# Moving the operands of a down-projection by 32 bytes in the on-chip memory

## The chip, the cores and the metric

The kernel runs on one core of a Trainium2 chip. The metric is the device time of one execution in microseconds (us); the time before is the median of three runs. Beside the runs there is one profiled execution, whose trace gives every duration used below. PE is the matrix engine (TensorE), PEld its weight loads, DVE the vector engine, ACT the scalar engine, POOL the GpSimd engine, SP the engine that issues most DMAs.

## The reference

One inference step of one trunk layer, for a prompt of 2048 tokens and a sample of 64 tokens (2112 in all), model width 1024. What matters here is the second half of the layer, a gated feed-forward block with a short causal convolution and a down-projection from 2816 to 1024 columns:

```python
h2 = rmsnorm(x, g2) * (1 + sc2) + sh2
up = h2 @ w_up                                   # 1024 -> 2 * 2816
conv = b_conv + sum(w_conv[j] * upp[:, j:j + T] for j in range(3))
a, g = jnp.split(conv, 2, -1)
x = x + gt2 * ((jax.nn.silu(g) * a) @ w_down)    # 2816 -> 1024
y = rmsnorm(x, g_final)
```

The first half (pooling mixer, matrix memory, output projection) takes roughly the first 790 us of the span and does not touch the tiles of this change.

## The kernel before, in words

Numbers are float32. Every large product is made from three passes over a number split in a high and a low part (weight high by operand high, weight high by operand low, weight low by operand high; `PASSES` in the code). So an operand tile holds two planes, `[P, 2, width]`, plane 0 the high part and plane 1 the low part.

The tokens are worked through in three groups of 704 (`FT`), each as two halves of 352 (`FH`). For each group the 22 blocks of 128 hidden columns are made one after the other by `Pair.products` (seven products of 352 columns each, line L1594, from the operand tiles `hx`), then convolved and gated on DVE, ACT and POOL, and split by ACT and DVE into an operand tile `av` of the down-projection. The down-projection has two forms:

- `down` (L2160): a row block of the output over the columns 0 to 448 and 448 to 704 of the group (`ENDS`), that is, matmuls of 448 and of 256 columns; 816 of each. It is used for all parts of the first group and for the last part of the two other groups.
- `quad_down` (L2037): four hidden blocks at a time by a seven-product scheme, in matmuls of 352 columns; 1344 of them, in the second and third groups.

`down_end` and `rows_add` (L2009) add the products from PSUM to the residual rows `x0` to `x7`. At the very end `final_end` (L1920), called once for the columns before 448 and once for those behind, forms the final norm: column sums on PE (L1935), the reciprocal root in the small tile `rs` (L1891, L1893), its spreading (L1951) and the last products with the rows.

The order of the instructions on PE, ACT, DVE and POOL is written out by hand in this half of the kernel (`tc.manual_schedule`); DMAs are issued by SP.

Where the tiles lie: the pool `f2` is filled from the upper end of the on-chip memory downwards. It holds, in this order of address, `OC`, `x0` to `x3`, seven `av` tiles of 5632 bytes (22 times 256), `x4` to `x7`, and on top the buffers of `rs`, of which each takes 32 bytes. So the size of the `rs` buffers sets where all that lies below them begins. In the built program before, each `av` tile begins 160 bytes past a multiple of 256. Its two planes are 2816 bytes apart (11 times 256), and the second part of 256 columns of `down` begins 1792 bytes in (7 times 256), so all operands of L2160 begin at 160 as well. In the tiles of `quad_down` two operands of 352 columns (1408 bytes, five and a half times 256) stand behind each other in a plane: the lower begins at 160, the upper at 32 past a multiple of 256; 672 matmuls read the one kind, 672 the other.

For comparison, the other operands: a row of `hx` is padded so that its 352 columns begin 128 bytes past a multiple of 256 (`HX, HO = 2 * 384, 32`); the operands `hl` and `mx` of the first half begin on multiples of 256, and so do all the split weights `wt`.

Of the kernel before, what the change touches and what calls it, by code (L numbers as in the profile page):

```python
# [9 lines left out]
F32 = mybir.dt.float32  # L10
# [6 lines left out]
P = 128  # L17
# [47 lines left out]
def tile_layer(ctx: ExitStack, tc: tile.TileContext, xT, vecs, cst, rst, w_mod, w_ada, w_qkou, w_v, w_pool,  # L65
# [21 lines left out]
    def m2_ps():  # L87
        return bank("m2")
# [580 lines left out]
    def fscr(dt=F32):  # L669
        if dt in ("rb", "ssum"):  # L670
            return spare[0].tile([P, FT], F32, tag=dt, name=dt)
        return spare[0].tile([P, FT], dt, tag="fscr", name="fscr", bufs=4)
# [855 lines left out]
    f2 = fctx.enter_context(tc.tile_pool(name="f2", bufs=1, side="right"))  # L1528
# [357 lines left out]
    def stat_cols(ps, out, tiles):  # L1886

        nf = sum(1 for t in tiles if t == P)
        for (a, b, n) in ((0, nf, P), (nf, len(tiles), tiles[-1])):
            if a < b:  # L1890
                dve.tensor_scalar(out=out[:n, a:b], in0=ps[:n, a:b], scalar1=1.0 / D, scalar2=EPS,  # L1891
                                  op0=ALU.mult, op1=ALU.add)
                pool.tensor_tensor(out=out[:n, a:b], in0=out[:n, a:b], in1=half[:n, :b - a], op=ALU.pow)  # L1893
# [26 lines left out]
    def final_end(o, x3, sums, lo, hi):  # L1920

        w = hi - lo
        tiles = [(t, min(P, hi - t)) for t in range(lo, hi, P)]
        for _ in range(4 if lo == 0 else 0):
            yield
        ps = m2_ps()
        rs = f2.tile([P, 5], F32, tag="rs", name="rs", bufs=2)
        order = [(ti, i) for ti in range(len(tiles)) for i in range(len(sums))]
        if lo > 0:
            order.sort(key=lambda c: c[1])  # L1930
        if lo > 0:
            dve.memset(ps[:, :len(tiles)], 0.0)
        for ti, i in order:
            (t, n), (sq, base) = tiles[ti], sums[i]
            pe.matmul(ps[:n, ti:ti + 1], sq[:, t - base:t - base + n], ones[:, 0:1], start=(i == 0 and lo == 0), stop=(i == len(sums) - 1),  # L1935
                      skip_group_check=lo > 0)

        if lo > 0:
            late[0](YLATE)
        stat_cols(ps, rs, [n for (t, n) in tiles])  # L1940
        if lo > 0:
            late[0](KD)
        else:
            for _ in range(4):
                yield

        def spread():

            pb = m2_ps()
            for ti, (t, n) in enumerate(tiles):  # L1950
                pe.matmul(pb[:, t - lo:t - lo + n], rs[:n, ti:ti + 1].broadcast_to([n, P]), ident[:n, :n], start=True, stop=True)  # L1951
            return pb
        pb = spread()

        if lo > 0:
            pc, rb = spread(), fscr()
            act.activation(rb[:, :w], pc[:, :w], AF.Copy)
        YG = ((0, 1), (1, 3), (3, 5), (5, 6), (6, 8))
        y = {}
        for (a, b) in YG:  # L1960
            if a % 2 == 0 or b - a == 2:
                t = f1.tile([P, 2, HX], F32R, tag="hx", name="y", bufs=2 * len(BN)).bitcast(F32).rearrange(
                    "p a t -> p (a t)")[:, :3 * w].rearrange("p (k t) -> p k t", t=w)
                j = 0
            for k in range(a, b):
                y[k] = (t, j)
                j += 1

        def store(a, b):
            (nc.sync if a < 5 else nc.scalar).dma_start(  # L1970
                out=yT[a:b, :, o.t0 + lo:o.t0 + hi].rearrange("k p t -> p k t"), in_=y[a][0][:, y[a][1]:y[a][1] + b - a, :w])

        def rows(upto):
            while due and due[0] < upto:
                k = due.pop(0)
                dve.tensor_tensor(out=y[k][0][:, y[k][1], :w], in0=x3[k][:, lo:hi], in1=pb[:, :w], op=ALU.mult)
                for (a, b) in YG:
                    if b == k + 1:
                        store(a, b)
        due = list(range(KD))  # L1980
        if lo == 0:
            late.append(rows)
            for k in range(KD - 4):
                rows(k + 1)
                yield
                yield
            return
        for k in (6, 7):
            pool.tensor_tensor(out=y[k][0][:, y[k][1], :w], in0=x3[k][:, lo:hi], in1=rb[:, :w], op=ALU.mult)
        due[6:] = []  # L1990
        rows(KD)
        store(6, 8)
        yield
# [117 lines left out]
    for o in fgroups:  # L2111
        Bo = B[o.g]
        held = None
        for pi, part in enumerate(PARTS[o.g]):
# [99 lines left out]
            for secs in [(c,) for c in ENDS] if ends else (ENDS,):  # L2214
                sums = [(ssum, 0)]
                for n in range(NE, KD):
                    ps = [take() for _ in secs]
                    down(ps, rows[n], range(nf), secs, ends)
                    down_end(n, ps, secs)
                if ends:  # L2220
                    bg[0].append(final_end(o, x3, sums, *secs[0]))
# [92 lines left out]
```

## Time and profile before

| | us |
|---|---|
| median of 3 runs | 2173.73 |
| the runs | 2172.52 to 2175.91 |
| the profiled execution's own time | 2174.68 |
| its span, first to last instruction | 2172.9 |
| PE busy | 2151.4 (99%) |
| granted TensorE clock, mean | 0.998 |

In a group's row the figures are: times it occurs, busy time of the group (overlapping instructions counted once), mean length of one instruction, and idle time of the engine just before. Matmuls are pipelined: one of 352 columns is some 320 ns long in the trace while the next starts about 160 ns after it. What a stream of matmuls costs is the distance from one start to the next, called its pace here. It can be read from a row of the timeline, which gives the first start, the stretch to the last end, and the count: (stretch less the length of the last one) by (count less one).

### The profile page before, as it was taken

To read this page: it belongs to the slowest core of one execution; us is meant where nothing else is said; L and a number is where in the kernel's file an instruction comes from. 1 tells how busy PE (TensorE), PEld (TensorE's weight loads), DVE (VectorE), ACT (ScalarE), POOL (GpSimd) and SP (SyncE) were. 2 spreads that over 40 slices of the span, in tenths; PEclk is the share of its full clock that TensorE was granted. 3 is DMA by queue.
4 is the path that set the end of the run, shared out by engine and by line. 5 is a ranking of instruction groups with operands and counts; after the bars stand their busy time and mean duration, and the time that the engine had idled before them with its cause. 6 is when DMAs were issued, how large, how long until landed. Compare 5 with 4: busy or idle time off the path is not lost.

```text
span 2172.9 us, 38060 instructions
## 1 busy us (share of the span) xinstructions
PE 2151.4 (99%) x13553; PEld 2044.4 (94%) x13553; DVE 1634.9 (75%) x3040; ACT 1096.1 (50%) x2181; POOL 258.4 (12%) x475
## 2 busy tenths in 40 slices
PE   8999999999999999999999999999999999999998
PEld 7888888888899999999999999999999999999998
DVE  5878668667955778797967668888886597887874
ACT  4554335334333446464736445655655365565554
POOL 0010000001000201010101220100101321111112
PEclk9999999999999999999999999999999999999999
DMA  8987997987888477888967976666668675555542
GB/s 319 328 305 233 323 321 246 309 302 244 301 283 288 169 260 239 282 292 300 350 214 255 321 245 222 234 208 209 228 222 274 223 255 186 170 177 190 171 160 77
DMA packets 297351, 539.51 MB, mean 248 GB/s; under 512 B 25760, under 2 KB 114336, under 8 KB 297160
## 3 DMA queue, kind: packets, MB, share of 16 engines
q1 hardware_dynamic: 286568, 511.87, 69.6%
q10 hardware_dynamic: 10592, 25.20, 3.0%
q8 instruction: 107, 1.75, 0.3%
q14 instruction: 84, 0.69, 0.1%
HBM read 410.98 MB, written 125.98 MB: 247 GB/s over the span
## 4 chain that ended last, share of the span: by engine, by line
PE 85%; DMA 5%; DVE 5%; issue 2%; ACT 2%; SPq 0%; POOL 0%; DVEq 0%; ACTq 0%; POOLq 0%
PE mm L1594 34%; PE mm L478 22%; PE mm L2160 12%; PE mm L2037 8%; PE mm L1133 3%; DVE wt L414 1%; DMA wt<-wsum 1%; PE m L1323 1%; DMA hl_kept<-wt 1%; PE m L1308 1%; PE m L1343 1%; PE m L1345 1%; DVE tg L1572 1%; DMA raw<-w_qkou 0%; ACT wt L411 0%
## 5 line engine op out<-in xcount | busy, mean ns | idle before, releaser
L1594 PE MATMUL mm<-hx,wt 128*128 128x352 f32 x5544 | 885.9, 321 | 0.7 <-DVE wt L414 0.5
L1594 PEld LDWEIGHTS mm<-hx,wt 128*128 128x128 f32 x5544 | 878.7, 188 | 2.6 <-DVE wt L414 2.0
L478 PE MATMUL mm<-hl,wt 128*128 128x512 f32 (+2 forms) x1920 | 387.4, 357 | 0.0
L411 ACT ACTIVATE wt<-raw 128x512 fp32r<-128x512 f32 (+3 forms) x470 | 276.6, 597 | 177.6 <-PE mm L478 52.8
L478 PEld LDWEIGHTS mm<-hl,wt 128*128 128x128 f32 x1920 | 316.4, 189 | 47.7 <-issue 4.4
L414 DVE TENSOR_TENSOR wt<-raw,wt 128x512 fp32r<-128x512 f32 (+3 forms) x470 | 312.8, 672 | 61.9 <-ACT wt L411 61.7
L2160 PE MATMUL mm<-av,wt 128*128 128x448 f32 (+1 forms) x1632 | 262.7, 322 | 0.0
L2160 PEld LDWEIGHTS mm<-av,wt 128*128 128x128 f32 x1632 | 250.4, 188 | 11.1
L2009 DVE SCALAR_TENSOR_TENSOR x<-mm,MOD,x 128x352 f32<-128x352 f32 (+3 forms) x360 | 167.5, 505 | 77.7 <-PE mm L2160 64.3
L2037 PE MATMUL mm<-av,wt 128*128 128x352 f32 x1344 | 220.7, 323 | 1.9 <-DVE x L2009 0.7
L2037 PEld LDWEIGHTS mm<-av,wt 128*128 128x128 f32 x1344 | 215.4, 188 | 5.0 <-DVE ea L1603 3.0
L1641 ACT ACTIVATE mm<-mm 128x352 f32<-128x352 f32 x196 | 87.8, 448 | 233.7 <-PE mm L1594 177.1
L478 PE MATMUL mm<-mx,wt 128*128 128x512 f32 (+1 forms) x960 | 182.9, 352 | 0.3 <-DVE scr L250 0.3
L478 PEld LDWEIGHTS mm<-mx,wt 128*128 128x128 f32 x960 | 159.4, 188 | 23.0 <-PE mm L478 0.5
L1572 DVE SCALAR_TENSOR_TENSOR ta<-ea,V,ta 128x704 f32<-128x704 f32 (+1 forms) x132 | 125.7, 953 | 58.4 <-ACT ta L1567 54.4
L1572 DVE SCALAR_TENSOR_TENSOR tg<-eg,V,tg 128x704 f32<-128x704 f32 (+1 forms) x132 | 125.7, 952 | 56.8 <-ACT tg L1567 54.3
L414 DVE TENSOR_TENSOR wt<-wt 128x512 fp32r<-128x512 f32 x196 | 133.0, 685 | 12.8 <-ACT wt L411 12.7
L411 ACT ACTIVATE wt<-wt 128x512 fp32r<-128x512 f32 x196 | 119.2, 622 | 36.6 <-DMA wt<-wsum 35.7
L1550 POOL COPY ea<-UC 128x2 f32<-128x2 f32 x66 | 33.1, 501 | 506.2 <-DVE ta L1572 407.3
L1781 ACT ACTIVATE tg<-tg 128x704 f32<-128x704 f32 (+1 forms) x66 | 52.5, 795 | 71.8 <-DVE tg L1572 71.8
L1133 PE MATMUL mm<-wt,hl 128*128 128x256 f32 (+1 forms) x576 | 71.4, 284 | 0.0
L1133 PEld LDWEIGHTS mm<-wt,hl 128*128 128x128 f32 x576 | 70.4, 190 | 0.8 <-issue 0.6
(305 smaller groups left out, 2207.0 us busy)
## 6 DMA issues: line engine op xcount, KB each, us to landing
wt<-wsplit SPq DMA_DIRECT2D x132, 512.0 KB, 4.3
raw<-w_up SPq DMA_DIRECT2D x198, 256.0 KB, 3.8
wt<-hl_kept SPq DMA_DIRECT2D x96, 512.0 KB, 6.3
wt<-wsum SPq DMA_DIRECT2D x132, 256.0 KB, 5.0
wsplit<-wt SPq DMA_DIRECT2D x66, 512.0 KB, 5.1
w<-w_up SPq DMA_DIRECT2D x88, 256.0 KB, 4.4
wsum<-w SPq DMA_DIRECT2D x44, 512.0 KB, 5.9
Bd<-fscr ACTq DMA_DIRECT2D x56, 352.0 KB, 4.3
```

What stands on the lines that cost most here:

```text
L411: act.activation(u.w[:, 0, :u.n], u.raw[:, :u.n], AF.Copy)
L414: dve.tensor_tensor(out=u.w[:, 1, :u.n], in0=u.raw[:, :u.n], in1=u.w[:, 0, :u.n].bitcast(F32), op=ALU.subtract)
L478: pe.matmul(ps[bi][:, :hi - lo], U[:, a, k % 4 * P:(k % 4 + 1) * P], mv[k][:, b, lo:hi], start=(at == 0 and pi == 0), stop=(k == order[-1] ...
L1133: pe.matmul(ps[ti][:n, :cols], h[4 * kh + k4][:, b, lo:lo + n], U[:, a, k4 % 2 * cols:(k4 % 2 + 1) * cols], start=(kh == 0 and k4 == 0 and ...
L1550: pool.tensor_copy(ext[:, 0:2], UC[:, f, :])
L1572: dve.scalar_tensor_tensor(out=t[:, :E], in0=ext[:, j:j + E], scalar=wc(j, f), in1=t[:, :E], op0=ALU.mult, op1=ALU.add)
L1594: pe.matmul(bk.t[:, :FH], U[:, a, kc * P:(kc + 1) * P], Bo.at(nm, kc, b), start=(first and kc == 0 and pi == 0), stop=(kc == 3 and pi == 2 ...
L1641: act.activation(to.t[:, :FH], bk.t[:, :FH], AF.Copy)
L1781: act.activation(self.tg[:, :E], self.tg[:, :E], AF.Silu)
L2009: dve.scalar_tensor_tensor(out=x3[n][:, a:b], in0=bk.t[:, a - lo:b - lo], scalar=gt2(n, s), in1=x3[n][:, a:b], op0=ALU.mult, op1=ALU.add)
L2037: pe.matmul(bk.t[:, :FH], U[:, a, c:c + P], quad.put(op, m, b), start=(first and m == 0 and pi == 0), stop=(m == 1 and pi == 2), skip_grou ...
L2160: pe.matmul(bks[i].t[:, :hi - lo], U[:, a, k % 4 * P:(k % 4 + 1) * P], av[k][:, b, lo:hi], start=(k == 0 and (a, b) == PASSES[0]), stop=(k ...
```

## The change

The tile `rs` gets three buffers in place of two. It is allocated twice, so the third buffer is never used; it only takes 32 bytes at the top of the pool.

```diff
@@ -1924,7 +1924,7 @@ def final_end(o, x3, sums, lo, hi)
         for _ in range(4 if lo == 0 else 0):
             yield
         ps = m2_ps()
-        rs = f2.tile([P, 5], F32, tag="rs", name="rs", bufs=2)
+        rs = f2.tile([P, 5], F32, tag="rs", name="rs", bufs=3)
         order = [(ti, i) for ti in range(len(tiles)) for i in range(len(sums))]
```

In the built program `OC`, `x0` to `x7`, the `av` tiles (which also hold the raw quarter weights `qs` in the first group) and one of the two `rs` buffers begin 32 bytes lower; every other tile stays where it was. The operands of L2160 and the lower ones of L2037 now begin 128 past a multiple of 256, the upper ones of L2037 on a multiple of 256. No instruction, wait or DMA is added, removed or moved on any engine.

## The prediction

> **What bounds the kernel now.** The page comes first: its line of busy times says which engine fills the span.
>
> ```profile
> span 2172.9 us, 38060 instructions
> PE 2151.4 (99%) x13553; PEld 2044.4 (94%) x13553; DVE 1634.9 (75%) x3040; ACT 1096.1 (50%) x2181; POOL 258.4 (12%) x475
> ```
>
> PE is busy 99% of the span and no other computing engine above 75%. The change touches no instruction, only where some operands begin, so the question is which instructions read or write the shifted tiles and how long PE waits around them. The groups by line and form, and the list of what PE waited for between 858 and 2153 us (the stretch in which the shifted tiles are read by matmuls), give that:
>
> ```profile
> L2160 PE MATMUL mm<-av,wt 128*128 128x448 f32 x816 | 178.8, 363 | 0.0
> L2160 PE MATMUL mm<-av,wt 128*128 128x256 f32 x816 | 111.0, 280 | 0.0
> L2037 PE MATMUL mm<-av,wt 128*128 128x352 f32 x1344 | 220.7, 323 | 1.9 <-DVE x L2009 0.7 <-DVE wt L414 0.4 <-DVE ea L1603 0.3
> L1594 PE MATMUL mm<-hx,wt 128*128 128x352 f32 x5544 | 885.9, 321 | 0.7 <-DVE wt L414 0.5
> ...
> PE mm L2037 <- DVE x L2009: 0.7, 1, 0.7
> PE mm L1594 <- DVE wt L414: 0.5, 2, 0.3
> PE mm L2037 <- DVE wt L414: 0.4, 1, 0.4
> PE mm L2037 <- DVE ea L1603: 0.3, 1, 0.3
> ```
>
> The reader sees 2976 matmuls (816 + 816 + 1344) that read `av`, and PE idle for 0.0, 0.0 and 1.9 us before them: the stream is bound by its own pace, not by a supplier. The last part of the chain of waits agrees:
>
> ```profile
> 2111.97 3.87 PE mm L2160 x24
> 2115.84 1.90 PE mm L1594 x12
> 2117.74 34.92 PE mm L2160 x204
> ```
>
> So a nanosecond more or less per matmul of `av` goes to the end of the kernel nearly whole: 1 ns on all of them is 3.0 us. The measure of what counts: 0.2% of this kernel, 4.35 us, is about what a measurement of it can tell from no change.
>
> **The paces.** Rows of the timeline in stretches with one kind of matmul (start, stretch to the last end, form, count):
>
> ```profile
> 2130.96 17.97 PE L2160 MATMUL mm<-av,wt 128*128 128x448 f32 x89
> 2148.97 3.45 PE L2160 MATMUL mm<-av,wt 128*128 128x256 f32 x28
> 1331.03 14.25 PE L2037 MATMUL mm<-av,wt 128*128 128x352 f32 x88
> 1199.76 6.50 PE L1594 MATMUL mm<-hx,wt 128*128 128x352 f32 x40
> 174.94 25.32 PE L478 MATMUL mm<-mx,wt 128*128 128x512 f32 x111
> 588.00 5.68 PE L1133 MATMUL mm<-wt,hl 128*128 128x256 f32 x46
> 867.91 2.64 PE L2160 MATMUL mm<-av,wt 128*128 128x448 f32 x12
> 870.51 1.36 PE L2160 MATMUL mm<-av,wt 128*128 128x256 f32 x10
> ...
> L478 PE MATMUL mm<-mx,wt 128*128 128x512 f32 x576 | 131.3, 389 | 0.0
> ```
>
> Taking off the length of the last one (363, 280, 323, 321 and 389 ns by form; for L1133 I use 280 too) and dividing by the count less one:
>
> - 448 columns from 160 past a multiple of 256: (17.97 - 0.363) / 88 = 200.1 ns
> - 352 columns from 160 or 32: (14.25 - 0.323) / 87 = 160.1 ns
> - 512 columns from a multiple: (25.32 - 0.389) / 110 = 226.6 ns
> - 352 columns from 128 (`hx`): (6.50 - 0.321) / 39 = 158.4 ns
> - 256 columns from 160: (3.45 - 0.280) / 27 = 117.4 ns
> - 256 columns from a multiple (L1133): (5.68 - 0.280) / 45 = 120.0 ns
>
> The first three lie on one line. From 352 to 448 columns the pace grows by 40.0 ns, from 448 to 512 by 26.5 ns, both 0.415 ns a column, and what is left over at no columns is about 13.4 ns (160.1 - 352 x 0.4167). I call this the fixed part. For `hx`, with the same 352 columns but a start at 128, it is 11.7 ns, for the 256 columns from 160 it is 10.7 ns, for those from a multiple 13.3 ns. The last two rows of the fence are a stretch in which the same L2160 ran slower: (2.64 - 0.363) / 11 = 207.0 ns for 448 columns, fixed part 20.3 ns, and (1.36 - 0.280) / 9 = 120.0 ns for 256. So the fixed part is not a constant: rows of this trace show 10.7 to 20.3 ns, and the same start address (160) appears with 10.7, 13.4 and 20.3.
>
> **The change part by part.**
>
> *The third buffer.* It costs no instruction, and no wait goes: `rs` is allocated twice and had two buffers. Price 0.
>
> *The lower operands of L2037, 160 to 128: 672 matmuls.* The nearest row is exact: `hx` has 352 columns from 128 and the same kind of weights, and paces 158.4 ns. 672 x (158.4 - 160.1) = -1.1 us. Bounds: 0 if the pace of `hx` comes from something other than its start, -1.8 us if the fixed part falls to the 10.7 ns of the 256-column row.
>
> *The upper operands of L2037, 32 to 0: 672 matmuls.* No row has 352 columns from a multiple of 256. The 512-column row from a multiple has the fixed part that these matmuls already have. I take 0; bounds -1.8 us and, by the slow stretch, 672 x 6.9 = +4.6 us.
>
> *The 448-column matmuls of L2160, 160 to 128: 816.* No row has them at 128. The nearest by start is `hx`, whose fixed part is 1.7 ns below the line: 816 x -1.7 = -1.4 us. Bounds: -2.2 us (fixed part 10.7), +5.6 us (all at the 207.0 ns of the slow stretch).
>
> *The 256-column matmuls of L2160, 160 to 128: 816.* They are already below the line. With the start of `hx` they may stay (0) or go to the 120.0 ns of the row from a multiple, +2.1 us; the fixed part of `hx` would be 118.4, +0.8 us. I take 0, since nothing in the trace shows 256 columns from 128.
>
> *What else touches the shifted tiles.* ACT and DVE write `av`, DVE and POOL read and write `x`. Rows of the same size on shifted and unshifted tiles:
>
> ```profile
> L1813 DVE TENSOR_TENSOR av<-tg,av 128x704 fp32r<-128x704 f32 x32 | 28.3, 885 | 0.1
> L1786 DVE TENSOR_TENSOR tg<-ta,tg 128x704 f32<-128x704 f32 x28 | 24.8, 884 | 3.3 <-ACT tg L1781 3.3
> L1910 DVE SCALAR_TENSOR_TENSOR x<-x,V,rb 128x704 f32<-128x704 f32 x16 | 15.1, 946 | 0.0
> L737 DVE SCALAR_TENSOR_TENSOR fscr<-fscr,G,rb 128x704 f32<-128x704 f32 x8 | 7.6, 946 | 0.0
> ```
>
> 885 against 884 and 946 against 946 ns, although `fscr` begins on a multiple of 256 and `tg` at three other offsets: the start does not move these engines, and a nanosecond there would lie beside PE anyway. The DMAs into `x` and `qs` land long before use (no wait of PE above names them). Price 0; were a row operation of DVE slower, PE waits of the 0.7 us kind (L2037 on L2009) would grow first.
>
> *Sum.* -1.1 + 0 - 1.4 + 0 = -2.5 us against the profiled execution's own 2174.68 us, giving 2172.2. That execution lies 1.0 us above the median of the runs, so the median would be 2173.73 - 2.5 = 2171.2 us. What is late next if PE is this much faster: DVE's weight splits (the 0.5 and 0.4 us on L414 above); spread over 1300 us, 2.5 us does not reach them.
>
> The Trainium skill has a rule that speaks against any effect: "TensorE: Matmul & The Clock Gate", section "Back-to-back issue gap", gives the distance of two warm matmuls as columns divided by 2.4 plus 2.5 ns, with no term for where an operand begins. By it 352 columns would pace 149.2 ns and the change would be worth 0. The trace's column cost agrees with it (0.415 ns), its fixed part of 10.7 to 20.3 ns does not.
>
> **The rivals.**
>
> *No effect.* The fixed part has nothing to do with the start, and `hx` is faster for another reason (other tiles, other order of planes). For it: the start 160 stands beside three different fixed parts, and the starts 160 and 32 pace alike in L2037. Against it: the one stream that begins at 128 is the one 352-column stream below the line, with 5544 matmuls in it. Time: 2173.7. In the Trainium skill, "SBUF — State Buffer", section "Door 1: The DMA port swizzle", tells of lines of 16 bytes, within which accesses run at full rate; 160, 128, 32 and 0 are all multiples of 16, so this rule too makes no difference between them. No row here can show it.
>
> *Faster by more.* Once the start is on a multiple of 128, the streams on the line drop to the lowest fixed part that the trace shows, 10.7 ns: 1344 x -2.7 = -3.6 us in L2037 and 816 x -2.7 = -2.2 us for 448 columns, together -5.8 us: 2167.9. For it: `hx` at 128 has gone more than half of that way. Against it: the 512 columns from a multiple are on the line.
>
> *Slower.* The slow stretch shows that the stream of L2160 can run in a longer pace with nothing else changed. If the new starts put it there for good, 448 columns cost 816 x 6.9 = +5.6 us and 256 columns 816 x 2.6 = +2.1 us, less the 1.1 us of L2037: +6.6 us, 2180.3. It passes 0.2% once some seven tenths of the L2160 matmuls run so ((4.35 + 1.1) / 7.7). For it: the two paces, 200.1 and 207.0, exist side by side at the same start. Against it: the slow stretch is short and falls back on its own, and `hx` at 128 keeps its short pace in the row above.
>
> **How the numbers follow.** Forecast (-2.5 us, within 0.2%): 0.33. No effect (within 0.2%): 0.12. Faster by more: 0.31. Slower: 0.24. This gives faster 0.31, same 0.45, slower 0.24. The forecast's own range, from the bounds of its terms without the slow stretch, is -5.8 to +2.1 us; the range must take in the faster rival (2167.9, so 2167.0) and most of the slower one. Stopping at 2179.0 leaves out its far end, about 1 in 10, and below 2167 about as much. The likeliest case alone would be 2167.9 to 2175.8.
>
> **What would show it right or wrong.** In the profile after, the timeline rows of the same stretches: L2037 should show a mix of 158.4 and 160.1 ns (mean 159.3), L2160 some 198.4 ns for 448 columns and 117.4 for 256, `hx` unchanged at 158.4 and the 512 columns at 226.6. The busy time of the L2037 group should fall from 220.7 by about 1 us, that of L2160 (178.8 and 111.0 by form) by about 1.4 together. The forecast is wrong if the 448 columns pace 207 (slower), if all are near 197 and 157 (faster by more), if nothing moves (no effect), or if the time moves while these paces stand still, which would put the cause in a transfer or a row operation that I priced at 0.

## The result, and the profile after

The changed kernel takes 2181.19 us at the median of 7 runs (2176.14 to 2182.84), the kernel before 2173.35 us (2170.73 to 2175.91): a ratio of 1.0033, 95% interval 1.0024 to 1.0043. It is slower by some 7 to 8 us, where the prediction had -2.5 us. Two executions in the batches below, one of the kernel before (2345.53 us) and one with only L2160 moved to 128 (5509.18 us), took far longer than all others and are left out of every median and ratio.

The profiled execution after has a span of 2181.1 us, 8.2 us more than before. The groups by line and form, with busy time of the group behind the bar, then the mean length of one:

```profile
span 2181.1 us, 38060 instructions
L1594 PE MATMUL mm<-hx,wt 128*128 128x352 f32 x5544 | 892.5, 322 | 0.0
L2037 PE MATMUL mm<-av,wt 128*128 128x352 f32 x1344 | 220.0, 323 | 1.5 <-DVE x L2009 0.4 <-DVE wt L414 0.4
L2160 PE MATMUL mm<-av,wt 128*128 128x448 f32 x816 | 180.8, 366 | 0.0
L2160 PE MATMUL mm<-av,wt 128*128 128x256 f32 x816 | 112.1, 282 | 0.0
```

Against the rows of before: L2037 went down by 0.7 us, the 448 columns up by 2.0, the 256 columns up by 1.1. But the largest step is in L1594, +6.6 us, and L1594 reads `hx`, which the change does not move. PE still waits for nothing there. Adding up the distances from each matmul's start to the next gives the same account: L1594 +6.0 us, 448 columns +2.0, 256 columns +0.8, L2037 -1.1, all other matmuls +0.1 on balance, together 7.8 of the 8.2 us.

The paces, as in the prediction, from timeline rows after (start, stretch, form of the first, count):

```profile
2139.16 17.91 PE L2160 MATMUL mm<-av,wt 128*128 128x448 f32 x87
2157.63 3.00 PE L2160 MATMUL mm<-av,wt 128*128 128x256 f32 x24
1339.18 14.01 PE L2037 MATMUL mm<-av,wt 128*128 128x352 f32 x87
901.75 18.49 PE L1594 MATMUL mm<-hx,wt 128*128 128x352 f32 x110
1011.74 18.49 PE L1594 MATMUL mm<-hx,wt 128*128 128x352 f32 x110
1141.72 18.53 PE L1594 MATMUL mm<-hx,wt 128*128 128x352 f32 x116
1368.75 18.53 PE L1594 MATMUL mm<-hx,wt 128*128 128x352 f32 x116
```

Stretch less the last length, by the count less one: 204.0 ns for 448 columns (before 200.1), 118.3 for 256 (117.4), 159.2 for L2037 (160.1). The last four rows are the finding: the same L1594 paces (18.49 - 0.322) / 109 = 166.7 ns in the second and third long stretch of the first group and (18.53 - 0.322) / 115 = 158.3 ns from the fourth on. Before, the second and third ran at 158.3 too:

```profile
900.76 18.53 PE L1594 MATMUL mm<-hx,wt 128*128 128x352 f32 x116
1007.73 18.53 PE L1594 MATMUL mm<-hx,wt 128*128 128x352 f32 x116
```

So a stream of `hx` has two paces, a short one of 158.3 ns and a long one of 166.7. The two long stretches hold 408 and 492 matmuls; 900 x 8.3 ns = 7.5 us. Some 2 us of that were won back, since short breaks that stood in these stretches before are gone in the slower stream. The granted TensorE clock from 800 to 1250 us, where both stretches lie, is 1.00 in both traces, so a lower clock is not the reason.

Both paces were already there before the change; near the beginning of the first group 64 matmuls of `hx` ran in the long one:

```profile
793.85 10.82 PE L1594 MATMUL mm<-hx,wt 128*128 128x352 f32 x64
```

(10.82 - 0.321) / 63 = 166.7 ns. The prediction did not use this row.

### The profile page after: what moved, and what is told of

It is laid out like the page before. It is cut to its first block, busy times and chain, and to the rows that moved or that the text cites. A ratio compares the mean times of both kernels' runs of the same rounds, so it can differ in the third digit from the quotient of the medians.

```text
span 2181.1 us, 38060 instructions
## 1 busy us (share of the span) xinstructions
PE 2160.3 (99%) x13553; PEld 2053.1 (94%) x13553; DVE 1634.9 (75%) x3040; ACT 1096.4 (50%) x2181; POOL 259.6 (12%) x475
## 4 chain that ended last, share of the span: by engine, by line
PE 90%; DVE 4%; DMA 3%; issue 1%; ACT 1%; SPq 0%; POOL 0%; DVEq 0%; POOLq 0%; ACTq 0%
PE mm L1594 37%; PE mm L478 23%; PE mm L2160 12%; PE mm L2037 8%; PE mm L1133 3%; DVE wt L414 1%; PE m L1323 1%; PE m L1343 1%; PE m L1345 1%; DMA hl_kept<-wt 1%; PE m L1308 1%; DMA raw<-w_ada 1%; DVE tg L1572 0%; ACT tg L1567 0%; PE mm L1069 0%
## 5 line engine op out<-in xcount | busy, mean ns | idle before, releaser
L1594 PE MATMUL mm<-hx,wt 128*128 128x352 f32 x5544 | 892.5, 322 | 0.0
L1594 PEld LDWEIGHTS mm<-hx,wt 128*128 128x128 f32 x5544 | 886.5, 188 | 0.5 <-DVE wt L414 0.5
L2160 PE MATMUL mm<-av,wt 128*128 128x448 f32 (+1 forms) x1632 | 265.8, 324 | 0.0
L2160 PEld LDWEIGHTS mm<-av,wt 128*128 128x128 f32 x1632 | 251.7, 188 | 12.9
L2037 PE MATMUL mm<-av,wt 128*128 128x352 f32 x1344 | 220.0, 323 | 1.5 <-DVE x L2009 0.4
L2037 PEld LDWEIGHTS mm<-av,wt 128*128 128x128 f32 x1344 | 214.8, 188 | 4.6 <-DVE ea L1603 2.8
L478 PEld LDWEIGHTS mm<-mx,wt 128*128 128x128 f32 x960 | 159.3, 188 | 22.7 <-PE mm L478 0.2
```

What stands on the lines that cost most here:

```text
L478: pe.matmul(ps[bi][:, :hi - lo], U[:, a, k % 4 * P:(k % 4 + 1) * P], mv[k][:, b, lo:hi], start=(at == 0 and pi == 0), stop=(k == order[-1] ...
L1594: pe.matmul(bk.t[:, :FH], U[:, a, kc * P:(kc + 1) * P], Bo.at(nm, kc, b), start=(first and kc == 0 and pi == 0), stop=(kc == 3 and pi == 2 ...
L2037: pe.matmul(bk.t[:, :FH], U[:, a, c:c + P], quad.put(op, m, b), start=(first and m == 0 and pi == 0), stop=(m == 1 and pi == 2), skip_grou ...
L2160: pe.matmul(bks[i].t[:, :hi - lo], U[:, a, k % 4 * P:(k % 4 + 1) * P], av[k][:, b, lo:hi], start=(k == 0 and (a, b) == PASSES[0]), stop=(k ...
```

## The experiments

One theory, A, stood against three rivals at first. A: the start of an operand within 256 bytes sets the pace of its own stream, and a stream of `hx` goes on in the phase in which the stream before it left PE. Rivals: the place of the tiles in the memory as such (B), the operands of L2037 or the rows `x` (C), or work that runs beside the `hx` stream and is slowed by the new places (called A2 below).

The experiments ran in three batches on different chips, each with the kernel before beside it; ratios are against the kernel before of the same batch, whose median was 2174.35, 2175.90 and 2174.53 us. Paces come from one profiled execution of each kernel, times from 4 to 11 executions.

In the experiments on one kind of operand, each `av` tile is 256 bytes longer, so that its start can be chosen by use, while all other tiles move by multiples of 256 bytes only:

```diff
+    def av_tile(name, off):
+        t = f2.tile([P, 2 * FT + 64], F32R, tag="av", name=name, bufs=AVB)
+        return t[:, off:off + 2 * FT].rearrange("p (a t) -> p a t", a=2)
```

`split_hi` (operands of L2160) and `Quad.put` (of L2037) take their own `off`, in steps of 8 numbers (32 bytes) from a base at 160; `x0` to `x7` stay at 160.

**All tiles 256 bytes lower.**

```diff
-        rs = f2.tile([P, 5], F32, tag="rs", name="rs", bufs=2)
+        rs = f2.tile([P, 5], F32, tag="rs", name="rs", bufs=10)
```

> Ten rs buffers in place of two: all shifted tiles lie 256 bytes lower than before, with the same starts past a multiple of 256 (160 and 32). Theory A (the pace of the matmul streams is set by the start of the operand within 256 bytes, and by the pace in which a stream is entered): all paces as before, the hx stretches of the first group at 158.3 ns, about 2173.4 us. Rival B (the place of the tiles in the memory as such, or the number of buffers, matters): slower than before as the change is, 2181 us.

Measured: 2175.46 us, ratio 1.0002 (0.9993 to 1.0012). The mean distance of starts, breaks left out, was 201.2 ns for 448 columns and 117.5 for 256, and the three `hx` stretches were entered at 158.3 (the first of them took up 166.7 for its last hundred matmuls, behind one distance of 197 ns, without a change in what it reads). The place as such and the number of buffers do nothing; rival B falls.

**Only the operands of L2160 at 128, and only those of L2037 at 128 and 0.**

```diff
-            self.d = f2.tile([P, 2, FT], F32R, tag="av", name="av", bufs=AVB)
+            self.d = av_tile("av", 56)        # only L2160; Quad.put has 0
...
-                self.tiles[key] = f2.tile([P, 2, FT], F32R, tag="av", name="av", bufs=AVB)
+                self.tiles[key] = av_tile("av", 56)     # only L2037; split_hi has 0
```

> Only the operands of L2160 begin at 128 past a multiple of 256; those of L2037 stay at 160 and 32, and x0 to x7 at 160. Theory A (L2160 at 128 paces worse itself, and leaves PE in the long pace when the hx stretch behind it begins): nearly the whole loss, hx at 166.7 ns in the two long stretches of the first group, 448 columns at 203.7 ns on the mean, 2179 to 2182 us. Rival C (the loss comes from the operands of L2037 or from the shifted rows x): 2172 to 2175 us.

> Only the operands of L2037 begin at 128 and 0 past a multiple of 256; those of L2160 stay at 160, and x0 to x7 at 160. Theory A: hx as before at 158.3 ns, L2160 as before at 201.2 ns for 448 columns, L2037 at 160 ns (half at 159), about 2172 to 2174 us. Rival C (the loss comes from the operands of L2037): 2179 to 2182 us.

Measured: only L2160, 2180.72 us, ratio 1.0030 (1.0017 to 1.0044), which is the whole loss with L2037 and `x` unmoved; only L2037, 2174.45 us, ratio 1.0001 (0.9992 to 1.0010). Rival C falls. In the trace of the first, L1594 took 4.9 us more than before, the 448 columns 2.0 and the 256 columns 0.9. In the second run L2037 went from 160.2 to 159.7 ns on the mean, breaks left out, and the `hx` stretches were entered in the short pace, though two of them took up the long one later.

The trace of the first of the two shows more than was asked. Its second long stretch, with idle time and its releaser in brackets:

```profile
897.60 4.16 PE L1594 MATMUL mm<-hx,wt 128*128 128x352 f32 x24
902.00 44.29 PE L1594 MATMUL mm<-hx,wt 128*128 128x352 f32 x278 [0.25 <-ACT mm L1641]
946.51 16.78 PE L1594 MATMUL mm<-hx,wt 128*128 128x352 f32 x100 [0.22 <-DVE wt L414]
946.78 3.80 PE L1594 MATMUL mm<-hx,wt 128*128 128x352 f32 x23
950.80 12.49 PE L1594 MATMUL mm<-hx,wt 128*128 128x352 f32 x74
```

24 matmuls pace (4.16 - 0.322) / 23 = 166.9 ns; then PE waits 0.25 us, and the next 278 pace (44.29 - 0.322) / 277 = 158.7. Here the pace changed across a break. Then PE waits 0.22 us, but that break does not bring the long pace back. The last two rows are narrower windows of the third: behind the break 23 matmuls still pace (3.80 - 0.322) / 22 = 158.1, then one distance between starts is 207 ns, with no idle time on record, and from there the pace is (12.49 - 0.322) / 73 = 166.7. The operands' places are the same throughout this stretch. The pace of `hx` is a state of the stream and not a property of its operands alone.

What switches it is not settled. In the thirteen traces with `hx` at 128, 67 places inside `hx` stretches have a distance of more than 190 ns between two starts, with at least eight matmuls on either side (places closer than ten matmuls counted as one). Behind 56 of them the short pace goes on. The longest wait among these, in the run with only the operands of L2037 moved, is ahead of this row:

```profile
1066.29 15.96 PE L1594 MATMUL mm<-hx,wt 128*128 128x352 f32 x99 [0.80 <-DVE wt L414]
```

Its mean distance is (15.96 - 0.322) / 98 = 159.6 ns, with one of 265 right behind the wait. Behind ten of the 67 places the long pace follows the short one: seven have distances of 194 to 265 ns and no idle time on record, three have 0.18 to 0.57 us of it. Behind one, the wait of 0.25 us above, the short pace follows the long. With only L2160 at 128 the long pace also begins at 1477 us with no distance over 170 ns near it.

**The changed kernel with a break ahead of the stretch.**

```diff
             b1 = self.b1 = take()
+            if o.g == 0 and f > 0 and self.i == 0:
+                for _ in range(4):
+                    pe.matmul(b1.t[:, 0:1], ones, ones[:, 0:1], start=True, stop=True)
```

> The changed kernel with four one-column products on PE, of a tile of ones into the bank about to be overwritten, ahead of the first product of each of the three hx stretches of the first group that follow a down-projection; some 0.4 us each. Theory A1 (the pace is a state that a stream inherits from what ran before it, and a break in the stream ends it): the two long hx stretches run at 158.3 ns in place of 166.7, that is 900 matmuls by 8.3 ns, -7.5 us, less 1.3 us for the products and some 2 us of waits that come back: 2176 to 2178 us. Rival A2 (the hx stream is slower there because of what runs beside it, such as writes into the av tiles on their new places): still 166.7 ns, 2182 us.

Measured: 2179.85 us, ratio to before 1.0027 (1.0018 to 1.0036), above the 2176 to 2178 us that A1 gave. In time alone this is not to be told from the changed kernel, so the answer rests on the trace of one execution. The break and the stretches behind it:

```profile
900.65 0.95 PE L1715 MATMUL mm<-ones_r 128*128 128x1 f32 x8
904.72 18.53 PE L1594 MATMUL mm<-hx,wt 128*128 128x352 f32 x116
1011.69 13.62 PE L1594 MATMUL mm<-hx,wt 128*128 128x352 f32 x85
```

Both stretches run at 158.3 ns ((18.53 - 0.322) / 115 and (13.62 - 0.322) / 84), with `av` still at 128. The third stretch was entered in the short pace as well. So in this execution the long pace went with what PE ran just before, and writes into `av` beside the stream did not bring it about; A2 falls as far as the trace goes. L1594 in all was 6.4 us shorter than in the changed kernel. The three breaks cost some 0.9 us each where I had expected 0.4 (a one-column product is two matmuls in the trace, 0.1 us each), which leaves some 3.7 of the 6.4; the span was 3.1 us shorter.

**A sweep of the start of L2160's operands**, with `off` of `split_hi` at 24, 32, 40, 48, 8 and 16.

> Only the operands of L2160 moved, to multiples of 256 (before: 160). Theory A1 (what counts is whether the start is a multiple of 64 bytes; 160 is not, 128 is): like the start at 128, 448 columns at some 203 to 207 ns, hx at 166.7 in one or both long stretches of the first group, 2178 to 2182 us. Theory A2 (128 is special, a multiple of 256 is in step like the 512-column stream, fixed part 13.3 ns): 448 columns at 200.0 ns, hx at 158.3, 2173 to 2175 us.

> Only the operands of L2160 moved, to 32 past a multiple of 256. Theory A1: as at 160, 448 columns at 200.0 ns, hx at 158.3, 2173 to 2175 us. Rival D: 2178 to 2182 us.

> Only the operands of L2160 moved, to 64 past a multiple of 256. Theory A1 (a multiple of 64): like the start at 128, 448 columns at some 203 to 207 ns, hx at 166.7 in one or both long stretches, 2178 to 2182 us. Theory A2 (128 alone is special): as before, 2173 to 2175 us.

> Only the operands of L2160 moved, to 96 past a multiple of 256. Theory A1 (no multiple of 64, as 160 is none): 448 columns at 200.0 ns in steady stretches, 256 columns at 117.3, hx at 158.3, 2173 to 2175 us. Rival D (160 alone is good by chance, every other start is worse): 2178 to 2182 us.

> Only the operands of L2160 moved, to 192 past a multiple of 256. The runs at 0, 32, 64, 96, 128 and 160 gave 202.8, 205 to 207, 200.0, 205.3, 203.9 and 200.0 ns for 448 columns. Theory E (what counts is the start within 128 bytes): as at 64, 448 columns 200.0 ns, 256 columns 113.3 ns, some 2171 us. Rival F (each start within 256 bytes has its own pace): anything else, 2173 to 2190 us.

> Only the operands of L2160 moved, to 224 past a multiple of 256. Theory E (the start within 128 bytes): as at 96, 448 columns 205.3 ns, 256 columns 119.9 ns and hx at 166.7 ns in the three long stretches of the first group, 2189 to 2192 us. Rival F: another pace, 2172 to 2185 us.

Measured (mean distance of starts of all 816 each, breaks left out; the fourth column counts which of the second, third and fourth long `hx` stretches were entered at 166.7 ns in the profiled execution; some of the others took that pace up behind a later break):

| start past a multiple of 256 | 448 columns, ns | 256 columns, ns | entered long, of 3 | median, us | before in the same batch, us | ratio to before |
|---|---|---|---|---|---|---|
| 0 | 203.4 | 119.5 | 0 | 2178.69 | 2175.90 | 1.0012 (1.0000 to 1.0024) |
| 32 | 205.0 | 116.8 | 0 | 2177.57 | 2175.90 | 1.0009 (0.9998 to 1.0021) |
| 64 | 200.1 | 114.1 | 0 | 2171.38 | 2175.90 | 0.9981 (0.9968 to 0.9994) |
| 96 | 205.2 | 119.5 | 3 | 2191.63 | 2175.90 | 1.0067 (1.0050 to 1.0084) |
| 128 (only L2160) | 203.7 | 118.8 | 2 | 2180.72 | 2174.35 | 1.0030 (1.0017 to 1.0044) |
| 160 (before) | 201.2 | 117.5 | 0 | 2174.35 to 2175.90 | the same | 1 |
| 192 | 201.9 | 114.0 | 3 | 2185.76 | 2174.53 | 1.0046 (1.0028 to 1.0064) |
| 224 | 204.0 | 118.3 | 1 | 2182.21 | 2174.53 | 1.0036 (1.0021 to 1.0050) |

The lines of the two ends and of 192, which splits the two effects:

```profile
2127.03 17.56 PE L2164 MATMUL mm<-av,wt 128*128 128x448 f32 x87
2145.06 3.22 PE L2164 MATMUL mm<-av,wt 128*128 128x256 f32 x27
```

```profile
2148.61 18.03 PE L2164 MATMUL mm<-av,wt 128*128 128x448 f32 x87
1144.73 18.50 PE L1594 MATMUL mm<-hx,wt 128*128 128x352 f32 x110
```

```profile
2163.74 3.11 PE L2164 MATMUL mm<-av,wt 128*128 128x256 f32 x26
904.80 18.49 PE L1594 MATMUL mm<-hx,wt 128*128 128x352 f32 x110
```

(The line numbers moved by four with the helper.) At 64: 200.0 and 113.1 ns. At 96: 205.4 ns, and `hx` at 166.8; there the distances add up to +11.3 us in L1594, +3.2 for 448 and +1.5 for 256 columns, -0.7 in L2037, together 15.3 of the 15.7 us by the medians. At 192: 256 columns at 113.2 ns, as good as at 64, and yet 11 us slower than before, with `hx` entered at 166.7 in all three stretches.

No simple rule holds. A multiple of 64 is not what counts (A1 of this sweep: 64 is the best start, 128 and 192 are slower than 160, and 32 and 96, which are no multiples of 64, pace 205 and not 200). 128 is not special (A2: at 0 the 448 columns pace 203.4 and not 200.0). The start within 128 bytes does not settle it either (E: 64 and 192 agree on 256 columns but not on the `hx` stretches, 96 and 224 on neither the stretches nor the time). D falls with 64. The ratios at 0 and 32 are hardly to be told from 1. What is left is F, that each start has its own pace; it named no pace and could hardly fail, so it is what remains and not a rule that was put to a test.

Nor does the start alone say how the stream behind is entered: at 128 two of three stretches were entered long, one short. In both traces at 128 the 256-column matmuls just ahead of the two follow each other at some 115, 118, 122, 120 and 119 ns in turn (in the changed kernel; within 2 ns of that with only L2160 moved), those ahead of the third at 120, 122 and 118. So the stream ahead has more than one state too, and the `hx` stream behind differs with it. That the one makes the other is argued here, not shown.

**The other operands at 64.**

In the first of two kernels `split_hi` and `Quad.put` both take `av_tile("av", 40)`; in the second `split_hi` alone does, and

```diff
-HX, HO = 2 * 384, 32
+HX, HO = 2 * 384, 16
```

> The operands of L2160 at 64 and those of L2037 at 64 and 192 past a multiple of 256. If 64 is a good start for 352 columns too (fixed part 6.7 ns as for the 256 columns at 64): L2037 at 153.3 ns on up to all of its 1344 matmuls, up to -9 us, 2162 us. If 352 columns behave as at the other starts: 158 to 160 ns, 2169 to 2172 us. If L2037 falls into the long pace: 166.7 ns, 2180 us.

> The operands of L2160 at 64 as in d64, and hx at 64 in place of 128 past a multiple of 256. If 64 lowers the fixed part of 352 columns to 6.7 ns: hx at 153.3 ns, 5544 matmuls by -5.0 ns, -28 us, 2143 us. If hx at 64 is in step with a whole 13.3 ns: 160.0 ns, +9 us, 2180 us. If it is in the long pace: 166.7 ns, +46 us, 2217 us.

Measured: L2037 at 64 and 192 as well, 2170.30 us, ratio 0.9985 (0.9976 to 0.9995), its matmuls at 159.9 ns; not to be told from L2160 alone at 64, but both are better than the kernel before and the changed one. `hx` at 64: 2180.91 us, ratio 1.0028 (1.0016 to 1.0040), and this line:

```profile
904.80 18.41 PE L1594 MATMUL mm<-hx,wt 128*128 128x352 f32 x114
```

(18.41 - 0.322) / 113 = 160.1 ns. It ran at 160.0 in every stretch of the span, also in the 64 matmuls near its beginning that pace 166.7 in the trace of before. So `hx` at 64 has one pace where `hx` at 128 has two. Against the short pace throughout, that is 5544 x 1.7 = 9.4 us; in the traces L1594 takes 7.4 us more than in the kernel with both others at 64 (888.2 against 880.8), whose `hx` stretches have breaks and some 80 matmuls in the long pace, and the medians of these two, of one batch, differ by 10.6 us. The fixed part of 6.4 ns that 256 columns reach at 64 is not to be had for 352 columns there.

## Why the prediction was wrong, point by point

**What bounds the kernel: right.** PE stays busy 99%, and what the paces lost came out at the end nearly whole (7.8 of 8.2 us).

**The third buffer, DVE, ACT, DMAs at 0: right.** Moving everything by 256 bytes changed nothing, with `x` unmoved the loss was the same, and the DVE row that writes `av` (L1813) went from 885 to 886 ns.

**L2037, lower -1.1 us, upper 0: right in sign, its size partly luck.** The distances add up to -1.1 us, and the row shown went from 160.1 to 159.2 ns, as forecast 159.3. But over all stretches the mean, breaks left out, went from 160.2 to 159.7 only, which is -0.7 us; the rest is shorter waits (1.9 to 1.5 us idle). Two of the eight stretches pace 160.8 and 160.9, more than before.

**L2160, 448 columns, -1.4 us: wrong in sign.** +2.0 us. I had taken the fixed part of `hx` at 128 and carried it to 448 columns at 128. The sweep shows that a fixed part can't be carried from one width to another: at 64 it is 6.4 ns for 256 columns (113.1 less 106.7) and 13.3 for 448 and for 352. The same holds for the 256 columns, put at 0, +0.8 us measured.

**`hx` unchanged: the step that failed.** It was not even a term of the sum; it stood among the signs to look for ("`hx` unchanged at 158.4 and the 512 columns at 226.6"), on the strength of one row of 40 matmuls. The sum priced only matmuls that read a shifted tile. L1594, which reads none, cost 6.0 us of the 8.2: 900 matmuls of two stretches at 166.7 ns in place of 158.3, less the breaks that went. The trace of before had shown that pace is a state: 207.0 and 200.1 ns at the same start for L2160, which the prediction used as a price, and 166.7 and 158.3 for `hx`, which it did not see.

**The slower rival: right in kind, wrong in place.** It named a longer pace taken up for good, priced at +6.6 us. The long pace came, but in L1594, and L2160 itself went to 204, not to 207; that its 2180.3 us lies near the measured 2181.19 is luck. The range, which stopped at 2179.0, left out the measured time.

**No effect, and the rule of the Trainium skill.** The gap that the Trainium skill gives in "TensorE: Matmul & The Clock Gate", section "Back-to-back issue gap", has no term for the start. The runs disagree: with the same instructions, starts 32 bytes apart (64 and 96) move 256 columns from 114.1 to 119.5 ns and 448 from 200.1 to 205.2. That section calls the formula the gap of an isolated matmul and gives other figures for streams of weight loads and matmuls, so the 149.2 ns of the prediction asked more of it than it says. The 16-byte lines of the Trainium skill, "SBUF — State Buffer", section "Door 1: The DMA port swizzle", don't separate these starts either; all eight are multiples of 16.

What stays open is why a start has its pace and what makes a stream go from one pace to the other. The runs show the paces, that moving the operands of L2160 alone brings the loss, and that with a break ahead of the `hx` stretches they were entered short; no record in the trace shows what happens inside PE.

## What to carry to other kernels

Where PE is the bound, look at the distance from start to start in several stretches of the same line, not at one: if it has two values with the same operands, the stream has a state, and an edit elsewhere can switch it. The start of a moving operand is then a setting to be swept with the whole kernel timed, since the best start for one width was not the best for another, and the stream that pays may be one that was not touched. Here the start at 64 in place of 160 for two widths of 816 matmuls each brought 0.2% (ratio 0.9981, 0.9968 to 0.9994), the start at 96 cost 0.7%.

## What the runs showed of the hardware that I had not expected

- A steady stream of alternating weight loads and matmuls can keep either of two paces for hundreds of matmuls: 158.3 or 166.7 ns at 352 columns and a start at 128, each over 492 matmuls without a change. Breaks of up to 0.80 us mostly left the pace as it was; one of 0.25 us went with the only change from long to short inside a stretch, and most changes from short to long came with no idle time on record, at one distance of 194 to 265 ns.
- The pace depends on where the moving operand begins within 256 bytes, in steps of 32 bytes, by up to 5 ns of 200 and 5.5 of 119, with no order in it that the eight starts show.
- The runs of one and the same kernel spread by several microseconds (the kernel before from 2170.35 to 2182.34 in one batch). One long stretch in the other pace is 3 to 4 us (408 or 492 by 8.3 ns), and this may be a part of it. Another part lies ahead: the first L1594 starts at 789.8 to 796.2 us in the thirteen traces with `hx` at 128, although no edit changes the work before it. So the sums by line are a better price of an edit here than the span of a single trace.
